# A fused decoder block: four row blocks normalised in place and transposed ahead of the last rows of the output projection

## The chip, the cores and the metric

The kernel runs on one core of one Trainium2 chip. The metric is device microseconds of one execution. The times come from three executions of the kernel before; the profile comes from one further execution, whose own time is given beside its span.

## What is computed

The input is 1024 tokens of width 1024 in float32. The block adds two attention branches (a sliding-window one and a top-k one) behind sigmoid gates, multiplies the mix by a 1024 x 1024 output projection, adds that to the residual, and then runs a gated feed-forward layer of hidden width 2816 and a last norm. The part that matters here, from the reference:

```python
    mixed = gate_a * (o_a @ w_branch_a[l]) + gate_b * (o_b @ w_branch_b[l])
    h = h + mixed @ w_out[l]
    hn = rms_norm(h, ffn_norm_g[l])
    h = h + (jax.nn.silu(hn @ w_ffn_gate[l]) * (hn @ w_ffn_up[l])) @ w_ffn_down[l]
y = rms_norm(h, final_norm_g)
```

## The kernel before

**Numbers and products.** Each float32 operand is split into a high part (a cast, on ACT) and a low part (a subtraction, on DVE or POOL), and each product is three matmuls: high x high, high x low, low x high (`mm3`, L203, whose matmul is recorded as L194). The three large products of the block's second half use Strassen-Winograd: each operand is cut in four quadrants, and seven products m1 to m7 of quadrants or of sums of quadrants take the place of eight.

**The output projection** (`phase_mix`, L1169, and `winograd`, L1215). Its seven products run in the order m1, m5, m6, m3, m2, m7, m4. A product has 48 matmuls of 128 x 512: four chunks k of the inner dimension, four row blocks i of 128 tokens, three matmuls each. The accumulators are PSUM banks: m2 and m5 take the four banks of the pool `sp` (tile `s`), the others the four of `mm` (tile `ps`). When a row block has its last chunk, DVE adds the bank into `h1` (L1254). For all but m4 the loop has k outside and i inside, so that the four row blocks end together; for m4 it has i outside, so that row blocks 4, 5, 6 and 7 end one after the other. The operand parts of m4's left side lie in `fhl` (four buffers), those of the right side in `th` and `tl` (five each).

**The norm between the two layers.** `done` (L1198) is called when half a row of `h1` is final. It calls `squares` (L1264), which squares 512 columns on ACT with a running sum; the squared values themselves go to a scratch tile that nobody reads and that has the tag `fs`, the two buffers that `ffn_hidden` uses for its sums of weights. When the second half is done (row blocks 0 to 3 after m2, 4 to 7 in m4), it stores the row block to DRAM (L1201, the feed-forward layer's residual), and calls `norm_scaled` (L1283): `row_scale` (L1270) makes the factor of each token with a tiny DVE instruction, a power on POOL and two more tiny DVE instructions, and ACT scales the row block into `xs` (L1288), which has two buffers. `norm_transposed` (L1290), called one row block late, transposes `xs` on PE in eight 128 x 128 pieces into two `s` banks (L1297), and DVE multiplies each bank by the norm's gain into the feed-forward layer's quadrants `hb11`, `hb21` (tokens 0 to 511) or `hb12`, `hb22` (tokens 512 to 1023) (L1300). After m4, the row blocks still pending are transposed (L1211).

**The feed-forward layer** (`phase_ffn`, L1303, `ffn_hidden`, L1364). DVE first forms the quadrant sums t1 to t4 in four cuts of 128 tokens (L1319 to L1324). Then eleven rounds q of `ffn_hidden` each do seven products for the gate and the up matrix. `product` (L1396) takes weight parts (`weight`, L1377: cast L1392 on ACT, low part L1393 on DVE for q = 0 and on POOL later), then the operand parts (`operand`, L1342: four casts L1350 on ACT, four subtractions L1351 on DVE, made once and kept), then 24 matmuls. The first product is quadrant 11 in two `s` banks, the second quadrant 21 in two `ps` banks. The low part of quadrant 11 goes into the tile `spare`, that of quadrant 21 into the room of `hb11` itself (L1316), so it can be written only when t1, which reads `hb11` (L1321), is complete.

**What sets the order.** Each engine runs its own list of instructions in order. The kernel's text gives only the dependences and the program order; the lists are written by a scheduler that runs a model of the time while it compiles, and puts on each engine what it takes to be ready. `issue_after(x)` tells it that the instructions in the block must stand behind x in the list of x's engine; it is an order and makes no wait of its own.

Of the kernel before, what the change touches and what calls it, by code (L numbers as in the profile page):

```python
# [7 lines left out]
F32 = mybir.dt.float32  # L8
# [11 lines left out]
P = 128  # L20
D = 1024
KC = D // P
T = 1024
NB = T // P
# [79 lines left out]
class Program:  # L104
# [1064 lines left out]
    def phase_mix(self):  # L1169
        nc, I = self.nc, self.I  # L1170

        self.act_dram = {nm: [self.dr.tile([P, 512], F32, name=f"act{nm}_{k}") for k in range(NF // 2)]
                         for nm in ("11", "12", "22", "s1", "s2", "s3", "s4")}
        self.h1_dram = [self.dr.tile([P, D], F32, name=f"h1_dram{b}") for b in range(NB)]
        self.f_es, mes = ExitStack(), ExitStack()
        self.B, self.xs = {}, {}
        self.fwp = self.f_es.enter_context(self.pool("fwp"))
        xp = mes.enter_context(self.pool("mixed"))

        X, W = self.X, self.W = [{ij: xp.tile([P, 4, 512], F32, name=f"{nm}{ij}") for ij in ("11", "12", "21", "22")} for nm in "xw"]  # L1180
        for m in range(KC):
            nc.scalar.copy(X[f"1{m // 4 + 1}"][:, m % 4], self.mixed[m])
        with self.pool("merge", side="right") as gp:
            self.branch_b(1, gp)
        self.xh_es.close()
        self.psum(4, 4, 0, 0)
        bp = self.f_es.enter_context(self.pool("fb", side="right"))
        for ij in ("11", "21", "12", "22"):
            self.B[ij] = bp.tile([P, 4, 512], F32, name=f"hb{ij}", tag=f"b{ij}", bufs=1)
        self.bp = bp  # L1190
        hp = mes.enter_context(self.pool("h1", side="right"))
        self.open_h1(hp)
        for b in range(NB):
            with self.tc.issue_after(self.mixed_in):
                nc.sync.dma_start(self.h1[:, b, :], I["x"][0][P * b:P * b + P, :])
        self.rp = mes.enter_context(self.pool("ring", side="right"))

        def done(b, nh):  # L1198
            self.squares(b, nh)
            if nh == 0:  # L1200
                nc.sync.dma_start(self.h1_dram[b], self.h1[:, b, :])  # L1201
                self.norm_scaled(b)
                self.pending.append(b)
                if len(self.pending) > 1:
                    self.norm_transposed(self.pending.pop(0))

        self.pending = []
        banks = lambda name: [(self.sp if name in ("m2", "m5") else self.mm).tile(
            [P, 512], F32, name="s" if name in ("m2", "m5") else "ps", tag="s" if name in ("m2", "m5") else "ps") for _ in range(4)]
        self.winograd(X, W, 4, ("m1", "m5", "m6", "m3", "m2", "m7", "m4"), banks, done)  # L1210
        while self.pending:  # L1211
            self.norm_transposed(self.pending.pop(0))
        mes.close()

    def winograd(self, a, b, kc, order, banks, done=None):  # L1215

        nc = self.nc
        a, b, sums = dict(a), dict(b), {}  # L1220

        def combine(d, name, dst, x, y, op):
            for k in range(kc):
                nc.vector.tensor_tensor(d[dst][:, k], d[x][:, k], d[y][:, k], op=op)
            d[name] = d[dst]

        sub, plus = ALU.subtract, ALU.add
        for at, name in enumerate(order):
            if name == "m5":
                combine(a, "s1", "21", "21", "22", plus)  # L1230
                combine(b, "t1", "12", "12", "11", sub)
            elif name == "m6":
                combine(a, "s2", "s1", "s1", "11", sub)
                combine(b, "t2", "t1", "22", "t1", sub)
            elif name == "m3":
                combine(a, "s3", "11", "22", "s2", sub)
                combine(b, "t3", "11", "t2", "11", sub)
                combine(a, "s4", "s2", "12", "s2", sub)
                combine(b, "t4", "t2", "t2", "21", sub)
            an, bn, old, to = WINOGRAD[name]  # L1240
            ps4 = sums[name] = sums[old] if old else banks(name)
            ops = []
            rows = name == "m4" and done
            for k in range(kc):
                ops.append((self.parts(a[an][:, k], self.fwp, ("fhl",), 4, False), self.parts(b[bn][:, k], self.rp, ("th", "tl"), NTH, False)))
            for k, i in [(k, i) for i in range(4) for k in range(kc)] if rows else [(k, i) for k in range(kc) for i in range(4)]:
                c = slice(P * i, P * i + P)
                x, y = ops[k]
                self.mm3(ps4[i], [(x[0][:, c], x[1][:, c], *y)], start=not old and k == 0, stop=k == kc - 1, skip_group_check=bool(old))
                if k < kc - 1:  # L1250
                    continue
                for half, nh, op in to:
                    h = self.h1[:, 4 * half + i, 512 * nh:512 * nh + 512]
                    nc.vector.tensor_tensor(h, h, ps4[i], op=op)  # L1254
                    if done and (name, half, nh) in (("m3", 0, 1), ("m2", 0, 0), ("m7", 1, 1), ("m4", 1, 0)):
                        done(4 * half + i, nh)
# [4 lines left out]
        self.h1 = hp.tile([P, NB, D], F32, name="h1")  # L1261
        self.ss = hp.tile([P, NB, 2], F32, name="ss")

    def squares(self, b, nh):  # L1264

        ss = self.ss[:, b, nh:nh + 1]
        junk = self.fwp.tile([P, 512], F32, name="sq", tag="fs", bufs=2)
        self.nc.scalar.activation(junk, self.h1[:, b, 512 * nh:512 * nh + 512], AF.Square, accum_out=ss)

    def row_scale(self, b):  # L1270
# [12 lines left out]
    def norm_scaled(self, b):  # L1283

        nc = self.nc
        r = self.row_scale(b)
        x = self.xs[b] = self.hp.tile([P, D], F32, name="xs", tag="xs", bufs=2)
        self.scaled_act = nc.scalar.activation(x, self.h1[:, b, :], AF.Copy, scale=r).ins  # L1288

    def norm_transposed(self, b):  # L1290

        nc, x = self.nc, self.xs[b]
        gcol = self.col["ffn_norm_g"]
        for kh in range(2):
            pt = self.sp.tile([P, 512], F32, name="s", tag="s")
            for k in range(4):
                nc.tensor.transpose(pt[:, P * k:P * k + P], x[:, 512 * kh + P * k:512 * kh + P * k + P], self.ident)  # L1297
            g = self.vec[:, gcol + 4 * kh:gcol + 4 * kh + 4]
            dst = self.B[f"{kh + 1}{b // 4 + 1}"]
            nc.vector.tensor_mul(dst[:, :, P * (b % 4):P * (b % 4) + P], pt.rearrange("p (k t) -> p k t", k=4),  # L1300
                                 g.unsqueeze(2).to_broadcast([P, 4, P]))
# [40 lines left out]
    def operand(self, name):  # L1342

        nc, hi = self.nc, self.Bhi[name]
        if name not in self.Blo:
            raw = self.B[name]
            pool, tag = next(self.places)
            lo = self.Blo[name] = pool.tile([P, 4, 512], F32R, name=f"l{name}", tag=tag, bufs=1)
            for k in range(4):
                nc.scalar.copy(hi[:, k], raw[:, k])  # L1350
                nc.vector.tensor_sub(lo[:, k], raw[:, k], hi[:, k].bitcast(F32))  # L1351
        return hi, self.Blo[name]

# [10 lines left out]
    def ffn_hidden(self, ap, q):  # L1364


        nc, I, wp = self.nc, self.I, self.fwp
        raws = [{}, {}]
# [25 lines left out]
            return hi, lo  # L1394

        def product(wname, bname, banks=None):  # L1396
            w = [weight(a, wname) for a in raws]
            first = banks is None
            if first:
                self.turn = not self.turn  # L1400
                pool, tag = (self.sp, "s") if self.turn else (self.mm, "ps")
                banks = [pool.tile([P, 512], F32, name=tag, tag=tag) for _ in range(2)]
            hi, lo = self.operand(bname)
            for k in range(4):
                for ps, (wh, wl) in zip(banks, w):
                    self.mm3(ps, [(wh[:, k], wl[:, k], hi[:, k], lo[:, k])], start=first and k == 0, stop=k == 3,
                             skip_group_check=not first)
            return banks
# [14 lines left out]
        def swiglu(pair, name, gate=None):  # L1423
# [4 lines left out]
            if name != "21":  # L1428
                nc.sync.dma_start(self.act_dram[name][q], act[name])

        x = product("11", "11")
        p1 = copies(x)
        swiglu(added(p1, product("12", "21")), "11")
        product("s2", "t2", x)
        u2 = copies(x)
        y = product("s1", "t1")
# [155 lines left out]
```

## Time and profile before

| | |
|---|---|
| Time of three executions | 1464.68, 1469.76, 1470.12 us, median 1469.76 |
| Time of the profiled execution | 1467.04 us |
| Its span in the trace | 1465.3 us, 21198 instructions |
| Its mean granted TensorE clock | 0.979 |
| Busy share | PE 94%, DVE 68%, ACT 56%, POOL 43% |

Of the times in the trace, 0 is the start of the span. m7 ends and the first transposes begin at 788.27 us, the last matmul of m4 starts at 802.73 us, and the first product of the feed-forward layer starts at 817.91 us. A busy PE is a stream of matmuls whose records overlap: the spacing from start to start is what counts, 0.23 us for a 128 x 512 one at full clock.

### The profile page before, as it was taken

Reading aid. Unit: us, or ns where it says so; the run is one execution under the profiler, and the core shown is the slowest. Engines: PE = TensorE matmul, PEld = TensorE weight load, DVE = VectorE, ACT = ScalarE, POOL = GpSimd, SP = SyncE. Lnnn points to the kernel's source line nnn. Section 1 sums busy time; section 2 is a strip of 40 time slices with the busy share of each in tenths; the row PEclk is TensorE's granted clock in tenths of the full one; section 3 lists DMA queues with packets and bytes.
Section 4 is the critical chain, followed back from the end, with each engine's and each line's share of the span. In section 5 each row is a group of like instructions: output and inputs, shape, how many; then the busy total and the mean of one; then the engine's idle time right before and its main releaser. Section 6 shows DMA issues by size and latency. Waiting matters only on the chain.

```text
span 1465.3 us, 21198 instructions
## 1 busy us (share of the span) xinstructions
PE 1380.8 (94%) x6847; PEld 1150.7 (79%) x6847; DVE 991.8 (68%) x2013; ACT 817.3 (56%) x1743; POOL 635.0 (43%) x895
## 2 busy tenths in 40 slices
PE   4999999986998999999899799999999999999997
PEld 3888988764876879898677678888888888888886
DVE  6257937959786797786797975444454447696593
ACT  5337987973786787884246633333333333444473
POOL 4225567474575666664101035555555554000005
PEclk9999999997998899999999899999999999999999
DMA  6511231463337564337902042333332328823332
GB/s 200 166 51 44 59 88 65 166 200 93 109 98 188 152 177 135 120 108 255 334 13 103 13 135 103 108 115 108 108 107 84 107 99 316 308 101 108 118 106 115
DMA packets 148038, 189.79 MB, mean 130 GB/s; under 512 B 11331, under 2 KB 95126, under 8 KB 147670
## 3 DMA queue, kind: packets, MB, share of 16 engines
q1 hardware_dynamic: 147568, 188.28, 39.7%
q8 instruction: 54, 0.88, 0.2%
q14 instruction: 58, 0.48, 0.1%
q10 hardware_dynamic: 198, 0.14, 0.0%
q0 software_dynamic: 160, 0.01, 0.0%
HBM read 133.49 MB, written 58.03 MB: 131 GB/s over the span
## 4 chain that ended last, share of the span: by engine, by line
PE 72%; DVE 11%; ACT 5%; issue 4%; DMA 4%; POOL 4%; SPq 0%; POOLq 0%; DVEq 0%; ACTq 0%
PE ps L194 28%; PE s L194 24%; PE gps L194 10%; PE pv L1085 2%; PE tp L1074 2%; PE s L1043 2%; ACT mask L891 2%; PE tp L199 1%; DMA ga<-gate_dram 1%; PE pv L194 1%; PE pv L1088 1%; POOL mask L835 1%; DMA gt<-ya_dram 1%; DMA da<-act 1%; POOL y L1553 1%
## 5 line engine op out<-in xcount | busy, mean ns | idle before, releaser
L1393 POOL TENSOR_TENSOR fhl<-fs,fhl 128x512 fp32r<-128x512 f32 x80 | 106.8, 1356 | 106.3 <-ACT fhl L1392 106.3
L1393 POOL TENSOR_TENSOR fhl<-fr,fhl 128x512 fp32r<-128x512 f32 x60 | 96.4, 1625 | 118.9 <-ACT fhl L1392 75.8
L194 PE MATMUL s<-ht,fhl 128*128 128x512 f32 x384 | 121.9, 392 | 0.6 <-DVE fhl L1393 0.6
L189 POOL TENSOR_TENSOR w_lo<-w_raw,w_hi 128x512 fp32r<-128x512 f32 x60 | 81.4, 1358 | 71.2 <-ACT w_hi L188 60.3
L194 PE MATMUL ps<-ht,fhl 128*128 128x512 f32 x320 | 100.8, 391 | 0.0
L194 PE MATMUL gps<-oh,w_hi 128*128 128x512 f32 x232 | 94.8, 409 | 5.1 <-ACT gt L949 4.8
L194 PE MATMUL gps<-oh,w_lo 128*128 128x512 f32 x232 | 92.7, 400 | 0.0
L194 PE MATMUL gps<-ol,w_hi 128*128 128x512 f32 x232 | 92.7, 399 | 0.0
L1463 ACT CAST yhl<-wd 128x512 fp32r<-128x512 f32 x66 | 41.1, 623 | 89.3 <-PE ps L194 50.2
L194 PE MATMUL s<-yhl,fhl 128*128 128x512 f32 x396 | 90.6, 389 | 0.0
L194 PE MATMUL ps<-yhl,fhl 128*128 128x512 f32 x396 | 90.3, 389 | 0.0
L194 PE MATMUL s<-h,fhl 128*128 128x512 f32 x272 | 87.5, 393 | 0.8 <-DVE hb L1300 0.5
L133 DVE TENSOR_TENSOR ptl<-tp,pth 128x512 fp32r<-128x512 f32 (+2 forms) x112 | 71.0, 646 | 23.7 <-ACT pth L127 23.4
L194 PE MATMUL ps<-h,fhl 128*128 128x512 f32 x256 | 82.8, 394 | 4.4 <-ACT h L1350 4.4
L194 PEld LDWEIGHTS s<-yhl,fhl 128*128 128x128 f32 x396 | 74.3, 188 | 15.5
L194 PEld LDWEIGHTS ps<-yhl,fhl 128*128 128x128 f32 x396 | 74.3, 188 | 15.5
L194 PEld LDWEIGHTS s<-ht,fhl 128*128 128x128 f32 x384 | 72.0, 188 | 17.9 <-DVE fhl L1393 1.0
L1392 ACT CAST fhl<-fr 128x512 fp32r<-128x512 f32 x66 | 39.9, 620 | 74.4 <-issue 32.9
L1464 DVE TENSOR_TENSOR yhl<-wd,yhl 128x512 fp32r<-128x512 f32 x66 | 45.6, 691 | 48.8 <-ACT yhl L1463 48.8
L891 ACT ACTIVATE mask<-high,smallg 128x1040 bf16<-128x1040 uint16 (+2 forms) x66 | 71.5, 1083 | 11.4 <-DVE high L836 5.4
L194 PE MATMUL s<-lt,fhl 128*128 128x512 f32 x192 | 75.4, 393 | 0.0
L1392 ACT CAST fhl<-fs 128x512 fp32r<-128x512 f32 x88 | 54.8, 625 | 35.8 <-PE s L194 17.4
(505 smaller groups left out, 4217.8 us busy)
## 6 DMA issues: line engine op xcount, KB each, us to landing
fr<-in_w_ffn_gate SPq DMA_DIRECT2D x22, 512.0 KB, 3.9
fr<-in_w_ffn_up SPq DMA_DIRECT2D x22, 512.0 KB, 4.7
wd<-in_w_ffn_down SPq DMA_DIRECT2D x44, 256.0 KB, 4.2
da<-acts SPq DMA_DIRECT2D x44, 256.0 KB, 3.1
w_raw<-in_w_in SPq DMA_DIRECT2D x40, 256.0 KB, 3.2
act<-a SPq DMA_DIRECT2D x33, 256.0 KB, 2.1
da<-act SPq DMA_DIRECT2D x33, 256.0 KB, 2.9
acts<-s SPq DMA_DIRECT2D x33, 256.0 KB, 2.0
```

Source lines behind the costliest of these rows:

```text
L133: b = nc.vector.tensor_sub(lo, ps, hi.bitcast(F32))
L189: (nc.vector if lo_dve else nc.gpsimd).tensor_sub(t[1], t[2], t[0].bitcast(F32))
L194: mm = self.nc.tensor.matmul(*args, **kw)
L199: mm = self.nc.tensor.transpose(*args)
L891: nc.scalar.activation(self.mask[j], src[j], AF.Sign, bias=at[:, i:i + 1], scale=scale, accum_out=out[:, i:i + 1])
L1043: nc.tensor.matmul(ps[:, :n], q[k][:, h, qc:qc + P], kb[:, h, at:at + n], start=k == 0, stop=k == 1)
L1074: mm = nc.tensor.transpose(pt[:, P * i:P * i + P], prs[par, e][:, NM + P * rr:NM + P * rr + P], self.ident)
L1085: mm = nc.tensor.matmul(acc[:, e, :], v, t[k][:, 256 * i:256 * i + 256], start=r + i + k == 0, stop=False)
L1392: nc.scalar.copy(hi, a[name])
L1393: (nc.gpsimd if q else nc.vector).tensor_sub(lo, a[name], hi.bitcast(F32))
L1463: nc.scalar.copy(hi, src)
L1464: nc.vector.tensor_sub(lo, src, hi.bitcast(F32))
```

## The change

Row blocks 0 to 3 are scaled in place in `h1`; `xs` stays for row blocks 4 to 7. The pending row blocks are transposed (`flush`) before m4's matmuls are written, and the matmuls of m4's row blocks 5, 6 and 7 (i = 1 to 3) are ordered on PE behind the last of these transposes; row block 4 (i = 0) is left free. The scratch of `squares` becomes a buffer of its own in this phase. In round q = 0, for the quadrants 11 and 21, the operand parts are written before the weight parts, and the casts of the weights are ordered on ACT behind the last cast of the operand.

```diff
         def done(b, nh):
-            self.squares(b, nh)
+            self.squares(b, nh, self.hp)
...
         self.winograd(X, W, 4, ("m1", "m5", "m6", "m3", "m2", "m7", "m4"), banks, done)
+        self.flush()
+        mes.close()
+
+    def flush(self):
         while self.pending:
             self.norm_transposed(self.pending.pop(0))
-        mes.close()
...
             rows = name == "m4" and done
+            if rows:
+                self.flush()
...
-                self.mm3(ps4[i], [(x[0][:, c], x[1][:, c], *y)], start=not old and k == 0, stop=k == kc - 1, skip_group_check=bool(old))
+
+                with self.tc.issue_after(self.transposed) if rows and i else nullcontext():
+                    self.mm3(ps4[i],     [(x[0][:, c], x[1][:, c], *y)], start=not old and k == 0, stop=k == kc - 1, skip_group_check=bool(old))
...
-    def squares(self, b, nh):
+    def squares(self, b, nh, pool=None):
...
-        junk = self.fwp.tile([P, 512], F32, name="sq", tag="fs", bufs=2)
+        junk = (pool or self.fwp).tile([P, 512], F32, name="sq", tag="sq" if pool else "fs", bufs=2)
...
-        x = self.xs[b] = self.hp.tile([P, D], F32, name="xs", tag="xs", bufs=2)
+        x = self.xs[b] = self.h1[:, b, :] if b < NB // 2 else self.hp.tile([P, D], F32, name="xs", tag="xs", bufs=2)
...
-                nc.tensor.transpose(pt[:, P * k:P * k + P], x[:, 512 * kh + P * k:512 * kh + P * k + P], self.ident)
+                self.transposed = nc.tensor.transpose(pt[:, P * k:P * k + P], x[:, 512 * kh + P * k:512 * kh + P * k + P], self.ident).ins
...
-                nc.scalar.copy(hi[:, k], raw[:, k])
+                self.act_split = nc.scalar.copy(hi[:, k], raw[:, k]).ins
...
-            w = [weight(a, wname) for a in raws]
+
+            ahead = q == 0 and bname in ("11", "21")
+            if ahead:
+                self.operand(bname)
+            with self.tc.issue_after(self.act_split) if ahead else nullcontext():
+                w = [weight(a, wname) for a in raws]
```

## Rows read from the trace of the kernel before

**Rows 1.** The page's busy time of each engine over the span.
```profile
PE 1380.8 (94%) x6847; PEld 1150.7 (79%) x6847; DVE 991.8 (68%) x2013; ACT 817.3 (56%) x1743; POOL 635.0 (43%) x895
```

**Rows 2.** Busy us by stage: PE, PEld, DVE, ACT, POOL; granted clock, DMA share, GB/s.
```profile
788.00:803.40 15.40, 15.13 (x82) 12.38 (x80) 12.25 (x22) 8.02 (x17) 0.26 (x1) 1.00 0.11 43
803.40:846.20 42.80, 31.70 (x135) 24.58 (x135) 42.42 (x81) 30.27 (x55) 4.40 (x4) 0.88 0.16 57
846.20:1240.00 393.80, 393.80 (x1715) 322.12 (x1716) 206.59 (x241) 137.03 (x245) 203.15 (x140) 1.00 0.36 123
1240.00:1275.00 35.00, 35.00 (x154) 28.64 (x153) 22.86 (x37) 14.64 (x26) 0.00 (x0) 1.00 0.97 358
```

**Rows 3.** Waits of PE from 846 us to the end: waited for, total, times, longest.
```profile
PE s L194 <- DVE fhl L1393: 0.6, 1, 0.6
```

**Rows 4.** PE in order of time, 803 to 827 us: idle before and its releaser in brackets.
```profile
807.48 1.22 PE L194 MATMUL ps<-h,fhl 128*128 128x512 f32 x2 [4.35 <-ACT h L1350]
810.71 5.62 PE L1297 MATMUL s<-ident,xs 128*128 128x128 f32 x28 [2.00 <-ACT xs L1288]
...
817.91 0.50 PE L194 MATMUL s<-h,fhl 128*128 128x512 f32 x1 [0.54 <-DVE hb L1300]
...
826.92 0.50 PE L194 MATMUL ps<-l,fhl 128*128 128x512 f32 x1 [3.26 <-DVE l L1351]
```

**Rows 5.** Stages inside that stretch, the same columns as rows 2.
```profile
807.40:810.60 3.20, 1.22 (x2) 0.50 (x2) 3.20 (x11) 3.20 (x8) 1.19 (x1) 0.50 0.00 1
810.60:817.90 7.30, 6.28 (x32) 5.68 (x32) 6.92 (x15) 3.39 (x4) 0.87 (x1) 0.68 0.00 0
...
823.70:826.90 3.20, 0.00 (x0) 0.00 (x0) 3.20 (x7) 3.20 (x7) 0.00 (x0) 1.00 0.00 0
```

**Rows 6.** DVE in order of time, 770 to 829 us.
```profile
773.49 0.69 DVE L133 TENSOR_TENSOR fhl<-x,fhl 128x512 fp32r<-128x512 f32 x1 [4.84 <-ACT fhl L127]
...
778.89 0.68 DVE L1254 TENSOR_TENSOR h<-h,s 128x512 f32<-128x512 f32 x1
...
792.35 0.69 DVE L1300 TENSOR_TENSOR hb<-s,vec 128x512 f32<-128x512 f32 x1
...
798.60 0.69 DVE L1300 TENSOR_TENSOR hb<-s,vec 128x512 f32<-128x512 f32 x1 [3.15 <-PE s L1297]
...
826.18 2.49 DVE L1351 TENSOR_TENSOR l<-hb,h 128x512 fp32r<-128x512 f32 x4
```

**Rows 7.** PE in order of time, 788 to 803 us.
```profile
788.27 1.91 PE L1297 MATMUL s<-ident,xs 128*128 128x128 f32 x16
...
798.63 1.47 PE L1297 MATMUL s<-ident,xs 128*128 128x128 f32 x12
...
802.73 0.40 PE L194 MATMUL ps<-th,fhl 128*128 128x512 f32 x1
```

**Rows 8.** ACT in order of time, 783 to 801 us.
```profile
783.91 2.19 ACT L1288 ACTIVATE xs<-h,rh 128x1024 f32<-128x1024 f32 x2
...
789.40 1.15 ACT L1288 ACTIVATE xs<-h,rh 128x1024 f32<-128x1024 f32 x1 [0.32 <-PE s L1297]
...
799.98 0.63 ACT L1268 ACTIVATE sq<-h 128x512 f32<-128x512 f32 x1 [6.54 <-DVE h L1254]
```

**Rows 9.** DMA of the row blocks' stores (L1201): 770 to 830 us, us to landing.
```profile
h_dram<-h SPq DMA_DIRECT2D x8, 512.0 KB, 3.4
```

**Rows 10.** Instructions of tile fs: ns min/median/max, first and last start.
```profile
L1382 DVE TENSOR_TENSOR fs<-fr x2: 683/687/691, 806.3 to 810.4; 128x512 f32<-128x512 f32 x2
```

**Rows 11.** SP's queue: the fourth and last load of round 0's weights.
```profile
715.95 1.29 SPq L1373 DMA_DIRECT2D fr<-in_w_ffn_up  x1
```

**Rows 12.** The stage 738 to 750 us, the same columns as rows 2.
```profile
738.00:750.00 12.00, 12.00 (x53) 9.66 (x52) 12.00 (x21) 5.36 (x10) 0.00 (x0) 1.00 0.00 0
```

**Rows 13.** ACT groups, 770 to 850 us: busy us, mean ns.
```profile
L1288 ACT ACTIVATE xs<-h,rh 128x1024 f32<-128x1024 f32 x8 | 8.9, 1142 | 1.9 <-PE s L1297 1.9
```

**Rows 14.** POOL in order of time: the power of the last row block.
```profile
810.65 0.87 POOL L1277 TENSOR_TENSOR rh<-rh,power 128x1 f32<-128x1 f32 x1 [2.06 <-DVE rh L1276]
```

## The prediction

> **What bounds the kernel now.** I read the page's busy shares first: PE is busy 94% of the span, so the place to look for time is where PE is not [rows 1]. The stage table finds it. In the stage behind the change, 846.2 to 1240 us, PE is busy all the time, as it is from 1240 to 1275, and from 846 us to the end of the span only one wait of PE is on record, 0.6 us at its very start [rows 2, 3]. In the stretch that holds the transition from the output projection to the feed-forward layer, 803.4 to 846.2 us, PE is busy 31.70 of 42.80 us, while DVE is busy 42.42 [rows 2]. So the transition is worth at most 42.8 - 31.7 = 11.1 us of idle PE and what the clock costs there, and whatever moves 846 us earlier moves the end by the same amount.
>
> PE's timeline says which waits those are: 4.35 us for a cast of a quadrant, 2.00 us for a scaled row block, some 0.9 us for banks that DVE had to empty, and 3.26 us for the low part of quadrant 21, the last wait to end [rows 4]. The clock adds a little: it was granted 0.50 and 0.68 after the first of these waits [rows 5], that is partly its lower level of 1.2 GHz, and 28 transposes took (5.62 - 0.27) / 27 = 0.198 us each there [rows 4] against (1.91 - 0.27) / 15 = 0.109 at 788 us [rows 7], 0.27 being the last one's own length: 28 x 0.089 = 2.5 us. The ceiling of any change to this stretch is then 11.1 + 2.5 = 13.6 us, 0.9% of the time.
>
> DVE's timeline says who decides. DVE has a hole of 3.15 us before 798.60 us, where it waits for the transposes of row blocks 2 and 3, and from there it is busy almost without a break until the low part of quadrant 21, four subtractions from 826.18 us [rows 6, 2]. That low part can't move up by itself: it is written over quadrant 11, so it stands behind t1, which needs row block 7. So **the end of DVE's list sets the end of PE's wait**, and the question is how much of DVE's work in 798.6 to 826.2 can be put where DVE is idle now. One DVE instruction of 128 x 512 counts (2.49 - 0.69) / 3 = 0.60 us in a run [rows 6].
>
> **The change part by part.**
>
> *Transposes of row blocks 0 to 3 ahead of the last rows.* Nothing is added: the same 32 transposes, eight gains (L1300) and 48 matmuls of m4 run. The gains of row blocks 2 and 3 are four of the sixteen and run from 798.6 us now, because PE's list has their transposes behind most of m4 [rows 7], though the scaling of row block 2 began at 789.40 us [rows 8]. With them ahead of row block 5 the four gains fall into the hole before 798.6 us: **4 x 0.60 = 2.4 us gained** of its 3.15. If the hole only wanders to where DVE waits for m4's later rows, it is 0; more than 3.15 it can't be.
>
> *PE behind the last transpose.* What is queued behind it is 36 matmuls of row blocks 5 to 7. The transposes need four `s` banks twice, so those of row blocks 2 and 3 wait for the gains of 0 and 1, which run on DVE from 792.35 us, behind the last additions of m7 [rows 6]. Three more and one low part of m4 between them, at 0.60, make the fourth bank free at about 795.4, and the last transpose ends at about 795.9. A matmul takes 393.8 / 1715 = 0.23 us in a full stream [rows 2], so the last of the 36 starts 35 x 0.23 = 8.05 us later, at about 803.95, against 802.73 now [rows 7]. PE pays 1.2 us in m4. It is covered by DVE's list, which is still the later of the two, and costs nothing unless it grows past the 2.4 us gained. The Trainium skill ("TensorE: Matmul & The Clock Gate", Part 3, The mechanism) says that matmuls start and end strictly in the order of the program, so none of the 36 could step around a waiting transpose; if they could, the 1.2 us would be nothing, and no run here shows which. I count them as held.
>
> *Scaling in place.* The third scaling waited 0.32 us for a transpose that read its buffer [rows 8]; that wait goes. What comes instead: a row block may be overwritten only when its store has been read out. The store takes 3.4 us [rows 9], and the last of the four row blocks is final on DVE at 778.89 + 0.68 = 779.6 us [rows 6], so the last store is through at about 783.0, before the first scaling of now, 783.91 us [rows 8]. Cost nothing; the cover is the chain of factors on DVE and POOL, and without it up to 3.4 us for the first row block. No DMA is added, and none changes its place in SP's queue by more than that.
>
> *Scratch of the squares.* Today the first sums of weights (L1382 and L1383, two instructions each, 0.60 us in a run) can't be written before the squares of the last rows leave the `fs` buffers, and stand from 806.3 us on, in the middle of DVE's full stretch [rows 10]. Their inputs are loaded long before: the last load was issued at 715.95 us, and from 738 to 750 us no DMA ran [rows 11, 12]. With `fs` free they can use the rest of the hole or the one of 4.84 us before 773.49 [rows 6]. Between 0 (the scheduler leaves them) and 4 x 0.60 = 2.4 us; I take 2.4, since nothing else claims these holes.
>
> *Casts ordered apart.* The eight casts of quadrants 11 and 21 can run in ACT's gap of 6.54 us before 799.98 [rows 8] instead of behind 803, where PE waits 4.35 us for one of them [rows 4]. The weights' casts, queued behind them, need `fhl` buffers that m4 frees only in its last row block, so they lose nothing. This shortens a chain that is not the last to end: after m4's end, row block 7 needs an addition of 0.68, a square of 0.63 [rows 8] with its read-out, the power of 0.87 [rows 14] with the tiny DVE work beside it, a scaling of 1.14 [rows 13], eight transposes (0.9 to 1.6) and two gains (1.3): 5.5 to 8 us, so it could be through at about 811, where the first product waits for a gain until 817.91 now [rows 4]. DVE's list behind it is longer than that. Alone 0, with a free DVE up to 8.
>
> *What is late next.* With the first product done at about 816, PE would wait for the low part of quadrant 21 longer than the 3.26 us of now, and the clock, which stayed at 1.00 through that wait [rows 5], may fall as it did after the 4.35 us. That costs between 0 and the 2.5 us found above; half of it can hide in DVE's list, and I take 0.8.
>
> Sum: 2.4 + 2.4 - 0.8 = **4.0 us gained**. The profiled execution took 1467.04 us, 2.7 under the median of 1469.76; on it the sum gives 1463.0, on the median 1465.8. The forecast is for the median: **1465.8 us**.
>
> **The rivals.**
>
> *The gain is two or three times that.* If the scheduler also puts the low part of quadrant 21 ahead of the sums t2 and t3 (eight instructions of 0.60 stand before it now), PE gets it 4.8 us earlier still: 4.0 + 4.8 = 8.8, 1461.0 us, with 13.6 as the limit, 1456.2. For it: row block 4 is free to finish before the transposes end, so that gains and sums for it can fill DVE in m4. Against it: t1 to t4 stand first in the program.
>
> *The hole wanders.* DVE finishes the gains early and then waits for m4's later rows, which end later than now; only the sums of weights are gained, and the clock takes most of that: 0 to 1.5 us, 1469 us. For it: between 798 and 804 us DVE would have only the additions, the tiny instructions and little else. This is also the case in which the scheduler's lists come out nearly as before.
>
> *Slower.* If DVE's list has five more instructions ahead of the gains of row blocks 0 and 1 (low parts of m4, the addition of row block 4, sums of weights), the fourth bank comes 5 x 0.60 = 3.0 us later, at 798.4. PE is out of work when the first 16 transposes and the 12 matmuls of row block 4 are done, at 788.27 + 1.7 + 12 x 0.23 = 792.7, and idles for most of 5.7 us, more than the 4.35 after which the clock fell [rows 4, 5], and the 36 matmuls start at the lower clock. The transposes ran 0.198 / 0.109 = 1.8 times as long there, which makes 0.42 us of a matmul's 0.23. The low clock lasted until the stage that ends at 817.9, some 10 us, so 20 of the 36 are 0.19 longer, 4 us: m4's last matmul starts at 798.9 + 8.05 + 4 = 811, 8 us late. Of DVE's tail 2.4 to 4.8 us has gone, so the low part of quadrant 21 comes 3.2 to 5.6 us later than now: 1473 to 1475.5 us, and more if DVE idles meanwhile. It decides from the point where m4 ends more than 4.8 us late. The strict order of matmuls that the Trainium skill states ("TensorE: Matmul & The Clock Gate", Part 3, The mechanism) would let none of the 36 run in that gap. Against it: the same gains ran at 792.35 in the present list.
>
> **How the numbers follow.** About 0.5% is what a measurement of this kernel can tell from no change: 7.3 us. Forecast 0.5 (1463 to 1468), larger gain 0.2, hole that wanders 0.2, slower 0.1. Faster by over 0.5% is under 1462.4: most of the larger gain, 0.17, and the low end of the forecast, 0.07, together 0.24. Slower by over 0.5% is over 1477.1: 0.06 of the last. Within: 0.70. The range takes in the larger gain down to 1458.5 and the wandering hole with the spread of three runs up to 1471.5.
>
> **What would show it.** Right: all 32 transposes of row blocks 0 to 3 between 788 and 796 us, no DVE hole before 798, m4's end at 804 to 805, the first sums of weights before 800, casts of quadrant 11 near 798, and a first low part of quadrant 21 at 821 to 823 with PE waiting for it. Wrong: that low part at 818 or earlier (larger gain); an idle DVE between 798 and 804 (the hole wandered); an idle PE of over 4 us with a clock under 0.8 between 788 and 804 (slower). A PE that waits again behind 846 us would break the premise that the rest only shifts.

## The result, and the profile after

| | before | after |
|---|---|---|
| Median (range, executions) | 1468.62 us (1462.1 to 1470.12, 9) | 1474.17 us (1472.51 to 1482.55, 9) |
| Ratio | | 1.0058, 95% interval 1.0043 to 1.0073 |
| Profiled execution | 1467.04 us, span 1465.3 | 1477.76 us, span 1476.0 |
| First transpose of the norm to the end of the span | 1465.3 - 788.27 = 677.0 us | 1476.0 - 789.85 = 686.2 us |

The change makes the kernel slower by 0.6%: the means of the executions lie 8.5 us apart (1475.74 and 1467.25), the medians 5.6. The last row is the measure used from here on, "the stretch to the end": the time ahead of the first transpose runs from 783.77 us (x6) to 790.90 us (x9) in the traces, though these two kernels have the same edits there. By it the change loses 9.1 us. It comes from one profiled execution of each kernel; beside the timed ratios it is off by up to 2.5 us (worst for x11 below), so differences smaller than that are not read from it alone.

Page of the kernel after, busy time of each engine (as [rows 1]):

```profile
PE 1384.0 (94%) x6847; PEld 1152.5 (78%) x6847; DVE 992.9 (67%) x2013; ACT 817.2 (55%) x1743; POOL 633.5 (43%) x895
```

The same instructions run, in nearly the same busy time. What changed is who waits. The stages of the kernel after, with the columns of [rows 2]; the first three are the same stretches, the fourth is the 58 us that begin at the first transpose, the fifth is discussed below:

```profile
788.00:803.40 15.40, 12.06 (x65) 9.00 (x63) 13.81 (x27) 7.61 (x18) 1.10 (x2) 0.98 0.13 52
803.40:846.20 42.80, 28.12 (x114) 22.34 (x115) 32.62 (x59) 24.79 (x46) 2.02 (x2) 0.77 0.08 31
846.20:1240.00 393.80, 393.58 (x1713) 321.13 (x1713) 203.92 (x247) 140.40 (x250) 197.79 (x136) 1.00 0.34 115
...
789.85:847.85 58.00, 39.98 (x178) 31.23 (x177) 46.22 (x85) 32.18 (x62) 3.12 (x4) 0.82 0.09 37
...
804.10:809.00 4.90, 4.90 (x16) 4.22 (x17) 1.38 (x2) 0.99 (x1) 0.00 (x0) 0.50 0.00 0
```

and the same 58 us of the kernel before:

```profile
788.27:846.27 58.00, 46.63 (x216) 36.89 (x214) 54.46 (x101) 38.02 (x71) 4.66 (x4) 0.91 0.14 54
```

PE idles 58.00 - 39.98 = 18.0 us there, against 58.00 - 46.63 = 11.4 before: 6.65 us more. Its mean granted clock is 0.82 against 0.91, and what is left of the loss, 9.1 - 6.65 = 2.5 us, is put down to PE's work running slower; that is an estimate. Behind 846 us PE is full in both, so the loss is made in this stretch and only passed on. The second thing to see is DVE: it was busy 42.42 of 42.80 us [rows 2] and is now busy 32.62. The engine that was to set the end has itself 10 us of idle time.

PE in order of time, kernel after (as [rows 4] and [rows 7]; L1304 are the transposes, and "xs" is a row block from 4 to 7):

```profile
789.85 1.91 PE L1304 MATMUL s<-ident,h 128*128 128x128 f32 x16
...
795.88 1.25 PE L1304 MATMUL s<-ident,h 128*128 128x128 f32 x8
...
804.10 1.97 PE L1304 MATMUL s<-ident,xs 128*128 128x128 f32 x8 [3.93 <-ACT xs L1295]
...
810.40 1.03 PE L1304 MATMUL s<-ident,xs 128*128 128x128 f32 x8
...
813.84 0.40 PE L194 MATMUL ps<-th,fhl 128*128 128x512 f32 x1
815.07 1.09 PE L1304 MATMUL s<-ident,xs 128*128 128x128 f32 x8 [0.83 <-ACT xs L1295]
820.77 1.32 PE L194 MATMUL ps<-h,fhl 128*128 128x512 f32 x2 [4.61 <-ACT fhl L1399]
...
830.35 1.97 PE L1304 MATMUL s<-ident,xs 128*128 128x128 f32 x8 [8.26 <-ACT xs L1295]
```

Row blocks 0 to 3 went as forecast: their last transposes end at 797.1 us, 7.3 after the first (7.6 were forecast). Then something that no step of the prediction has: the transposes of row block 4 stand in PE's list *between* m4's row blocks 5 and 6, those of row block 5 between 6 and 7. At 804.10 PE has waited 3.93 us for row block 4 to be scaled, with the 24 matmuls of row blocks 6 and 7 queued behind. Their operands were complete (the last low part of m4 starts on DVE at 796.34).

The edit itself puts the transposes there. Its order reads `self.transposed` anew for each row block, and `norm_transposed` writes that variable. When row block 5 is written, `done` calls `norm_transposed` for row block 4, so row block 6 is ordered behind the transposes of row block 4, and in the same way row block 7 behind those of row block 5. The section on the change says of all three row blocks that they stand behind the last transpose of row block 3; that holds for row block 5 alone. Without the order (the kernel before, x1, x4, x8, x11) the scheduler leaves the transposes of row blocks 4 to 7 behind m4.

m4's last matmul starts at 813.84 instead of 802.73 [rows 7]. The last wait, 8.26 us, is for row block 7, behind two matmuls of the feed-forward layer.

The chain of waits of the kernel after, 796 to 833 us (start, us, what), shows both parts at once:

```profile
797.13 2.82 PE ps L194 x12
...
799.97 0.70 DVE h L1261
...
800.75 0.73 ACT sq L1275 x2
...
801.87 0.56 POOL rh L1284
...
802.90 1.16 ACT xs L1295
...
804.10 1.97 PE s L1304 x8
806.07 4.49 PE ps L194 x12
810.56 0.87 PE s L1304 x8
811.43 2.82 PE ps L194 x12
...
814.28 0.69 DVE h L1261
...
826.39 0.14 DVE rh L1283
...
829.15 1.16 ACT xs L1295
...
830.35 1.97 PE s L1304 x8
```

**Part one, inside m4.** The chain is addition, square, tiny instructions with the power on POOL, scaling, transposes: about 4.1 us from 799.97 to 804.10, and PE has nothing else that its list lets it do. The clock falls: 804.10 to 809 us is granted 0.50, the level of 1.2 GHz. The price is in the same rows: 12 matmuls take 4.49 us at 806.07 and 2.82 at 811.43, eight transposes 1.97 and 0.87; 1.67 + 1.10 = 2.8 us.

**Part two, row block 7.** Its addition starts at 814.28, its transposes at 830.35, 16.1 us later, where the prediction gave a chain of 5.5 to 8 us to the end of its gains. ACT in order of time, kernel after, says what stood ahead of its square:

```profile
814.92 2.16 ACT L1357 CAST h<-hb 128x512 fp32r<-128x512 f32 x4
816.99 1.13 ACT L1399 CAST fhl<-fr 128x512 fp32r<-128x512 f32 x2
818.03 2.17 ACT L1357 CAST h<-hb 128x512 fp32r<-128x512 f32 x4
820.11 1.13 ACT L1399 CAST fhl<-fr 128x512 fp32r<-128x512 f32 x2
821.15 0.63 ACT L1275 ACTIVATE sq<-h 128x512 f32<-128x512 f32 x1
```

Twelve casts, so the square comes at 821.15, 6.2 us after the addition has ended. Then its first tiny instruction waits in DVE's list behind sums and low parts until 826.31, and the chain of waits from 814.28 to there runs along DVE's list. DVE in order of time, kernel after:

```profile
826.31 0.20 DVE L1283 TENSOR_SCALAR rh<-ss 128x1 f32<-128x1 f32 x1
```

### The profile page after: what moved, and what is told of

It is laid out like the page before. It is cut to its first block, busy times and chain, and to the rows that moved or that the text cites. A ratio compares the mean times of both kernels' runs of the same rounds, so it can differ in the third digit from the quotient of the medians.

```text
span 1476.0 us, 21181 instructions
## 1 busy us (share of the span) xinstructions
PE 1384.0 (94%) x6847; PEld 1152.5 (78%) x6847; DVE 992.9 (67%) x2013; ACT 817.2 (55%) x1743; POOL 633.5 (43%) x895
## 4 chain that ended last, share of the span: by engine, by line
PE 73%; DVE 9%; ACT 5%; DMA 5%; issue 4%; POOL 4%; SPq 1%; POOLq 0%; ACTq 0%; DVEq 0%
PE ps L194 28%; PE s L194 26%; PE gps L194 9%; PE pv L1085 2%; PE s L1043 2%; PE tp L1074 2%; ACT mask L891 2%; DMA ga<-gate_dram 1%; PE tp L199 1%; PE pv L194 1%; DVE pa L749 1%; POOL mask L835 1%; DVE ptl L133 1%; POOL y L1565 1%; PE pv L1088 0%
## 5 line engine op out<-in xcount | busy, mean ns | idle before, releaser
L1284 POOL TENSOR_TENSOR rh<-rh,power 128x1 f32<-128x1 f32 x16 | 11.0, 699 | 144.4 <-DVE rh L1283 144.4
```

## The experiments

Two theories after the trace. **Row order**: ordering m4's row blocks 5 to 7 behind the transposes is the loss, through part one and part two; the other edits cost nothing. **Casts** (the rival): ordering the first weights' casts behind the operands' casts puts them ahead of row block 7's square, so that edit is the loss. All kernels compute the whole reference. "Ratio" is the time over that of the kernel before on the same chip, with its 95% interval; "stretch" is from the first transpose to the end, 677.0 before and 686.2 with the change.

**x1, the change without the row order.**

```diff
-                with self.tc.issue_after(self.transposed) if rows and i else nullcontext():
-                    self.mm3(ps4[i],     [(x[0][:, c], x[1][:, c], *y)], start=not old and k == 0, stop=k == kc - 1, skip_group_check=bool(old))
+                self.mm3(ps4[i], [(x[0][:, c], x[1][:, c], *y)], start=not old and k == 0, stop=k == kc - 1, skip_group_check=bool(old))
```

> The changed kernel without the order that puts the matmuls of m4's row blocks 5 to 7 behind the last transpose of row block 3; all else stays. Theory ORDER (that order lets the transposes of row blocks 4 to 6 stand between m4's row blocks in PE's list, so that PE waits in the middle of m4 for a scaling that can't be ready): the loss goes, ratio 0.996 to 1.002, no wait of PE for xs before m4's last matmul, which starts at 802 to 805 us. Theory CASTS (the eight casts of quadrants 11 and 21 and the four of the weights stand ahead of row block 7's square on ACT): most of the loss stays, ratio 1.004 to 1.008, a wait of 6 to 9 us for the last xs.

Measured: ratio 1.0008 (0.9993 to 1.0022), stretch 676.7. PE in order of time:

```profile
806.12 1.32 PE L194 MATMUL ps<-h,fhl 128*128 128x512 f32 x2 [5.44 <-ACT fhl L1397]
808.30 6.58 PE L1302 MATMUL s<-ident,xs 128*128 128x128 f32 x32 [0.87 <-ACT xs L1293]
```

The whole loss goes. The transposes of row blocks 4 to 7 stand together behind m4, as before. And the other three edits together bring nothing that can be measured.

Twelve casts stand ahead of row block 7's square here too, with no loss. The square, and the last tiny instruction of that row block, on ACT and DVE:

```profile
806.49 0.63 ACT L1273 ACTIVATE sq<-h 128x512 f32<-128x512 f32 x1
```

```profile
808.50 0.16 DVE L1284 SCALAR_TENSOR_TENSOR rh<-rh 128x1 f32<-128x1 f32 x1
```

From the square's start to the finished factor takes 2.2 us here and 7.9 us with the change (821.15 to 829.05). So the casts by themselves are not part two. What x1 lacks is the gains and sums of row blocks 4 to 6 in DVE's list ahead of the tiny instructions; they came forward with the transposes of these row blocks.

**x2, the change without the order of the casts.**

```diff
-            ahead = q == 0 and bname in ("11", "21")
-            if ahead:
-                self.operand(bname)
-            with self.tc.issue_after(self.act_split) if ahead else nullcontext():
-                w = [weight(a, wname) for a in raws]
+            w = [weight(a, wname) for a in raws]
```

> The changed kernel with operand and weight parts in the old order. Theory ORDER: m4 is still cut in pieces, a wait of 3 to 5 us for xs inside m4, ratio 1.003 to 1.008. Theory CASTS: row block 7's square comes within 2 us of its addition, the wait of 8.26 us is under 3, ratio 0.997 to 1.002.

Measured: ratio 1.0070 (1.0049 to 1.0091), stretch 686.3. The waits for row block 4 and row block 7 are still there, 3.93 and 8.14 us. Twelve casts of weights and operands stand ahead of row block 7's square without this edit too. The rival falls: with or without it, the loss is there.

**x3, the kernel before with the row order alone** (and the `flush` that it needs; no scaling in place, no scratch, no order of casts).

```diff
+            if rows:
+                self.flush()
...
+                with self.tc.issue_after(self.transposed) if rows and i else nullcontext():
...
```

> The kernel before with only the early flush and the order on m4's row blocks 5 to 7: xs in two buffers, scratch in fs, casts as before. Theory ORDER: slower alone, ratio 1.003 to 1.009, PE waits inside m4. Theory CASTS: same as before, 0.998 to 1.002.

Measured: ratio 1.0073 (1.0052 to 1.0094), stretch 687.4. PE in order of time:

```profile
798.14 1.78 PE L1303 MATMUL s<-ident,xs 128*128 128x128 f32 x8 [2.63 <-ACT xs L1294]
...
824.01 1.97 PE L1303 MATMUL s<-ident,xs 128*128 128x128 f32 x8 [11.04 <-ACT xs L1294]
```

The row order alone makes the whole loss, with waits in the same two places, 2.63 and 11.04 us. The four kernels that have it and still call the transposes of row blocks 4 and 5 inside m4 (the change, x2, x3, x9) all wait there.

**x4, the kernel before with the squares' own scratch alone.**

```diff
-            self.squares(b, nh)
+            self.squares(b, nh, self.hp)
```

> The kernel before with only the squares' scratch in a buffer of its own. By the prediction's term the four first sums of weights leave DVE's full stretch: 0 to 2.4 us gained, ratio 0.998 to 1.000, first sums before 800 us. If the scratch costs (a tile that shifts others), 1.001 or more.

Measured: ratio 1.0001 (0.9989 to 1.0014), stretch 676.6. Tile `fs` (ns min/median/max, first and last start), and then PE's last wait:

```profile
L1382 DVE TENSOR_TENSOR fs<-fr x22: 677/694/1691, 725.2 to 1208.0; 128x512 f32<-128x512 f32 x22
```

```profile
828.98 0.50 PE L194 MATMUL ps<-l,fhl 128*128 128x512 f32 x1 [2.69 <-DVE l L1351]
```

The first sums of weights did leave DVE's full stretch, for 725 us, where they began at 806.3 [rows 10]. Of the 2.4 us that they free, PE gets 0.57 back: 3.26 us [rows 4] became 2.69. Most of the rest is new idle time of DVE. Two stretches with the columns of [rows 2], both from 15.28 us after the first transpose on, x4 and then the kernel before:

```profile
806.00:829.00 23.00, 12.63 (x59) 9.80 (x59) 21.00 (x45) 15.77 (x30) 3.30 (x4) 0.85 0.15 60
```

```profile
803.55:826.55 23.00, 13.25 (x58) 10.61 (x58) 22.62 (x48) 15.97 (x30) 4.25 (x4) 0.78 0.15 61
```

DVE idles 2.00 us in x4 and 0.38 before; it waits 0.35 us for a square, 0.73 for a power and 0.86 for transposes.

**x5, the change with the transposes of row blocks 4 to 7 ordered behind m4's last matmul.**

```diff
-                if len(self.pending) > 1:
+                if b < NB // 2 and len(self.pending) > 1:
...
-        self.flush()
+        with self.tc.issue_after(self.last_row):
+            self.flush()
...
-                    self.mm3(ps4[i],     [(x[0][:, c], x[1][:, c], *y)], start=not old and k == 0, stop=k == kc - 1, skip_group_check=bool(old))
+                    self.last_row = self.mm3(ps4[i], [(x[0][:, c], x[1][:, c], *y)], start=not old and k == 0, stop=k == kc - 1, skip_group_check=bool(old))
```

> The whole change, and the transposes of row blocks 4 to 7 ordered on PE behind m4's last matmul, so that none stands between m4's row blocks. Theory ORDER, in the form that the transposes between the rows cost: no wait of PE for xs before m4's last matmul, which starts at 803 to 806 us after a first transpose at 788; a wait for the last xs of 3 to 6 us stays, because the squares of row block 7 stand behind twelve casts on ACT; from the first transpose to the end 676 to 680 us (677.0 before, 686.2 with the change). If instead the 36 matmuls behind row block 3's transposes are what costs: 684 us or more.

With it `self.transposed` stays at the last transpose of row block 3 through all of m4, so row blocks 5 to 7 are ordered as the prediction had it. Measured: ratio 1.0022 (1.0012 to 1.0033), stretch 680.5. m4 is whole again, and 5.6 of the 9.1 us are back. PE, and then ACT, in order of time:

```profile
822.26 1.97 PE L1304 MATMUL s<-ident,xs 128*128 128x128 f32 x8 [5.34 <-ACT xs L1295]
```

```profile
813.15 0.63 ACT L1275 ACTIVATE sq<-h 128x512 f32<-128x512 f32 x1
...
821.06 1.15 ACT L1295 ACTIVATE xs<-h,rh 128x1024 f32<-128x1024 f32 x1 [6.16 <-DVE rh L1286]
```

What is left is part two: row block 7's square still stands behind twelve casts, its factor is ready 7.8 us after the square's start (2.2 in x1), and its transposes are waited for.

**x6, x5 with the casts of the operands ordered behind the last scaling on ACT.**

```diff
-            for k in range(4):
-                self.act_split = nc.scalar.copy(hi[:, k], raw[:, k]).ins
-                nc.vector.tensor_sub(lo[:, k], raw[:, k], hi[:, k].bitcast(F32))
+            with self.tc.issue_after(self.scaled_act):
+                for k in range(4):
+                    self.act_split = nc.scalar.copy(hi[:, k], raw[:, k]).ins
+                    nc.vector.tensor_sub(lo[:, k], raw[:, k], hi[:, k].bitcast(F32))
```

> As x5, and the casts of the feed-forward layer's operands ordered on ACT behind the last scaling, so that row block 7's square goes first. The wait for the last xs goes under 2 us; from the first transpose to the end 672 to 676 us, ratio 0.994 to 0.999. If DVE's list sets the end alone: 677, as before.

Measured: ratio 0.9984 (0.9973 to 0.9995), stretch 675.8. The rest of the loss goes, and the kernel is faster than before, by 0.16%; x7 and x10, which contain these edits, have intervals that reach past 1. PE in order of time:

```profile
809.43 1.97 PE L1304 MATMUL s<-ident,xs 128*128 128x128 f32 x8 [5.51 <-ACT xs L1295]
```

The wait for row block 7 was expected under 2 us and is no shorter than in x5, but it ends 25.7 us after the first transpose (at 783.77 us) instead of 32.6 (822.26 - 789.66), since none of the operands' casts stands ahead of it.

**x9, the change with only the second of these repairs**: the casts behind the last scaling, as in x6, and the transposes of row blocks 4 and 5 still inside m4, where the order of the change puts them.

```diff
-            for k in range(4):
-                self.act_split = nc.scalar.copy(hi[:, k], raw[:, k]).ins
-                nc.vector.tensor_sub(lo[:, k], raw[:, k], hi[:, k].bitcast(F32))
+            with self.tc.issue_after(self.scaled_act):
+                for k in range(4):
+                    self.act_split = nc.scalar.copy(hi[:, k], raw[:, k]).ins
+                    nc.vector.tensor_sub(lo[:, k], raw[:, k], hi[:, k].bitcast(F32))
```

> The whole change, with the transposes of row blocks 4 to 7 left free to stand between m4's rows as in the change, and only the casts of the operands ordered behind the last scaling on ACT. If the loss is two separate things (PE held by a transpose inside m4, and row block 7's chain behind casts), this repairs the second alone: PE still waits 3 to 4 us for a scaling inside m4, the wait of row block 7's transposes falls from 8.3 to 4 to 6 us, first transpose to end 680 to 683 us (before 677.0, the change 686.2), ratio 1.002 to 1.004. If the order on ACT is all that was wrong, it comes out as x6 did: 675 to 677 us, ratio 0.998 to 1.000. If transposes inside m4 are all that was wrong, 685 to 687 us.

Measured: ratio 1.0042 (1.0027 to 1.0056), stretch 681.8. PE in order of time:

```profile
805.15 1.97 PE L1303 MATMUL s<-ident,xs 128*128 128x128 f32 x8 [3.94 <-ACT xs L1294]
...
823.26 1.97 PE L1303 MATMUL s<-ident,xs 128*128 128x128 f32 x8 [7.05 <-ACT xs L1294]
```

By the stretches these are two separate losses: this repair alone gives 4.4 us, x5's alone 5.6, together 10.0, and x6 has 10.3. By the ratios it is less clear: the two give 2.3 and 5.3 us, x6 10.9, and the interval of x9 overlaps that of the change. The wait of 7.05 us was expected at 4 to 6: the square now starts at 815.04, but DVE's list still holds the tiny instructions back until 821.79.

**x7, x6 with t1 of all four cuts and the operands 11 and 21 written ahead of t2 to t4.**

```diff
+        self.operand("11")
+        self.operand("21")
+        for at, n in CUTS:
+            cut = {nm: B[nm][:, :, at:at + n] for nm in B}
...
```

> As x6, and t1 of all four cuts and the operand parts of quadrants 11 and 21 written ahead of t2, t3 and t4 in the program. If DVE's list is what PE waits for at the second product, 1 to 3 us better than x6 and a wait for the low part of quadrant 21 under 3 us; if the time is set by row block 7's chain, the same as x6.

Measured: ratio 0.9992 (0.9978 to 1.0006), stretch 675.2. PE's wait for row block 7 is the same 5.51 us, and a wait of 2.70 us for a cast of a weight comes behind it. No gain over x6.

**x8, x1 with room of its own for the casts of quadrant 11** (they are written to a tile whose room is given out when the projection's pools close), and four buffers instead of five for `th` and `tl` to make that room.

```diff
-NTH = 5
+NTH = 4
...
+        self.h11 = bp.tile([P, 4, 512], F32R, name="h11", tag="h11", bufs=1)
...
```

> As x1 (no row order), with the high part of quadrant 11 placed in the pool that is open during the projection, and the ring of th and tl cut from five to four buffers to make the room. Theory ROOM: the casts of quadrant 11 could not be scheduled ahead of m4's last matmul because their tile lies in the room of the projection's pools, handed out only when those close. Then here they run before 801 us where in x1 they run after 801; the time stays within 0.3% of x1, since the second product still waits for the low part of quadrant 21. If ROOM is wrong, the casts stay behind 801 us.

Measured: ratio 1.0008 (0.9998 to 1.0019), stretch 678.6. ACT in order of time:

```profile
801.45 2.18 ACT L1357 CAST h<-hb 128x512 fp32r<-128x512 f32 x4 [7.85 <-DVE hb L1306]
```

The casts start 12.5 us after the first transpose instead of 14.4 in x1 (800.26 - 785.83), right behind the gains that they need. So room was worth 2 us of lateness, and PE's time nothing. The expectation was a start before 801 us here and behind 801 us in x1; from the start of the span neither came true (801.45 and 800.26).

**x10, x6 with the sums t1 to t4 ordered on DVE behind row block 7's last tiny instruction.**

```diff
+        with self.tc.issue_after(self.scaled_dve):
+            for at, n in CUTS:
...
```

> x6 with the sums t1 to t4 ordered on DVE behind row block 7's last tiny instruction as well. In x6 that chain waits in DVE's list behind sums, and its transposes wait 5.5 us on PE. If DVE's order is the rest of that wait, it falls below 2.5 us, first transpose to end 672 to 675 us, ratio 0.995 to 0.998. If the sums that are put off come back as a later wait for t1's parts or a low part (the rival), that wait grows by 2 to 4 us and the time stays at x6's: 675 to 677 us, ratio 0.998 to 1.000.

Measured: ratio 0.9991 (0.9979 to 1.0002), stretch 675.7. PE in order of time, then two stages with the columns of [rows 2]:

```profile
808.23 1.78 PE L1304 MATMUL s<-ident,xs 128*128 128x128 f32 x8 [1.96 <-ACT xs L1295]
...
817.51 1.22 PE L194 MATMUL s<-h,fhl 128*128 128x512 f32 x2 [2.26 <-DVE fhl L1402]
```

```profile
802.00:808.20 6.20, 3.26 (x25) 2.57 (x24) 5.85 (x14) 4.30 (x7) 0.55 (x1) 1.00 0.46 183
808.20:822.50 14.30, 10.59 (x27) 6.97 (x28) 14.30 (x25) 11.24 (x22) 0.00 (x0) 0.52 0.00 0
```

The wait for row block 7 falls from 5.51 to 1.96 us, so DVE's order was most of what was left of it. The time does not follow: the low part of a weight, put off on a DVE that is busy all of the 14.30 us, is late by 2.26, and PE's work there runs at a granted clock of 0.52.

**x11, the kernel before with only the casts behind the last scaling.**

```diff
-            for k in range(4):
-                nc.scalar.copy(hi[:, k], raw[:, k])
-                nc.vector.tensor_sub(lo[:, k], raw[:, k], hi[:, k].bitcast(F32))
+            with self.tc.issue_after(self.scaled_act):
+                for k in range(4):
+                    nc.scalar.copy(hi[:, k], raw[:, k])
+                    nc.vector.tensor_sub(lo[:, k], raw[:, k], hi[:, k].bitcast(F32))
```

> The kernel before with only the casts of the operands ordered behind the last scaling on ACT; no row order, no own scratch, no scaling in place. If what x6 won comes from the chain's place on ACT alone, this gives it too: 674 to 676.5 us from first transpose to end, ratio 0.997 to 0.9995. If it needs the early transposes or the free scratch of the change, 676.5 to 679 us, ratio 0.9995 to 1.002.

Measured: ratio 0.9990 (0.9976 to 1.0003), stretch 678.0. The interval overlaps both expectations; the ratio itself is on the side of a gain, the stretch on the side of none. Whether x6's 0.16% needs the early transposes stays open.

## Why the prediction was wrong

The forecast was 1465.8 us and a gain of 4.0; the change is 0.58% slower, so the direction and the range were wrong, and "slower" had a chance of 0.1, slower by over 0.5% one of 0.06.

- **The step that failed is "PE behind the last transpose".** It says that what is queued behind the transposes "is 36 matmuls of row blocks 5 to 7" and that "PE pays 1.2 us in m4". That price is right for row blocks 0 to 3 (last transpose 7.3 us after the first). But only 12 of the 36 matmuls are queued there. The order takes its anchor from a variable that `norm_transposed` writes again inside m4, so row blocks 6 and 7 are queued behind the transposes of row blocks 4 and 5, each behind a chain of four engines. That costs 3.93 us of waiting, all of it for row block 4, and 2.8 us of lower clock, and m4's last matmul starts 24.0 us after the first transpose (813.84 - 789.85) instead of 14.5 (802.73 - 788.27). x5 takes these transposes out of m4 alone, and 5.6 us come back; x3 shows that the row order by itself puts them there. No run keeps the anchor at row block 3 and leaves the transposes of row blocks 4 and 5 free.
- **"Casts ordered apart" was right on its price and wrong on the chain.** The edit costs and gains nothing that can be measured (x1, x2). The casts did not run in ACT's gap ahead of m4's end either; against x1, x8 puts 2 us of that down to the room of their tile. But "a chain that is not the last to end", with row block 7 through at about 811 us, failed: it was costed as if ACT and DVE would run each of its steps at once. Twelve casts and a run of DVE work stand ahead of it in two lists, with m4 whole (x5) as with m4 cut up, and it ends last. With the casts alone ahead of it there is no loss (x1); with the casts put behind it the stretch is 4.4 us shorter (x9; 2.3 us by the ratio, not clear of the noise), and DVE's list still holds it. How much belongs to either list stays open. The trace of the kernel before already had a chain longer than the sum. Row block 7's addition on DVE and its scaling on ACT, kernel before:

```profile
804.11 0.69 DVE L1254 TENSOR_TENSOR h<-h,ps 128x512 f32<-128x512 f32 x1
```

```profile
814.47 1.15 ACT L1288 ACTIVATE xs<-h,rh 128x1024 f32<-128x1024 f32 x1 [0.56 <-PE s L1297]
```

  That is 10.4 us from the start of one to the start of the other, with the transposes and gains still to come, where 5.5 to 8 us were given for all.
- **"The end of DVE's list sets the end of PE's wait" held before and only in part after.** The gains of row blocks 2 and 3 fell into the hole, as said: they are through at 799.4 us, and the largest hole ahead of them from 787 us on is 1.21 us. DVE in order of time, kernel after:

```profile
787.95 4.87 DVE L1261 TENSOR_TENSOR h<-h,ps 128x512 f32<-128x512 f32 x8 [1.21 <-PE ps L194]
...
796.94 2.47 DVE L1307 TENSOR_TENSOR hb<-s,vec 128x512 f32<-128x512 f32 x4
```

  The hole did not close, it moved: DVE then waits for m4's late row blocks, and idles 42.80 - 32.62 = 10.2 us where it was full, before its list holds PE up again from 814.28 on, as the chain of waits shows. That is the rival "the hole wanders", and more.
- **The two gains of 2.4 us were over-sized even without the loss.** The scratch alone has a ratio of 1.0001 (x4), and scratch, scaling in place and order of casts together 1.0008 (x1). x6, with both gains, the loss repaired and the casts put last, has 0.9984, some 2.3 us of the 4.8. A DVE that is busy 42.42 of 42.80 us was not the only limit: when 2.4 us left its list, it idled 1.6 us more for a square, a power and transposes, and PE's wait shrank by 0.57 us (x4).
- **Scaling in place at nothing: right.** The four scalings run as one block of 4.27 us from 785.50, and x1 has them without a loss.
- **"What is late next", 0.8 us for the clock, was too small**: by the estimate above 2.5 us more than before.
- **The rival "slower" had the size, 1473 to 1475.5 us, not the place.** It has PE wait for banks ahead of the last transposes of row blocks 0 to 3; inside m4 PE's only long idle stretch is 3.93 us behind them. Its step from an idle PE to the lower clock and a late m4 is what happened.
- **The rule that was cited holds here.** The Trainium skill ("TensorE: Matmul & The Clock Gate", Part 3, The mechanism) has matmuls start and end strictly in program order, and the prediction had no row for it. Now there is one: at 804.10 PE had waited 3.93 us for eight transposes with 24 ready matmuls behind them, and none stepped around. Had they done so, they would have filled the wait (an estimate: 24 x 0.23 = 5.6 us).

## What to carry to other kernels

An order hint holds what its anchor variable names at that moment. Where a loop places the hint several times and the same loop writes the variable, each piece gets another anchor: write down for each piece which instruction it stands behind, and give that instruction the length of the chain it waits for. When the last part of a stage feeds a chain over several engines, cost that chain by its place in each engine's list and not by the sum of its steps, and look in the trace of the kernel before for how long it takes there. The two faults here came from one edit, and repairing one of them gave back 5.6 of 9.1 us (x5), so a repair that gives back a part is no sign of a wrong theory. And an engine that is busy 99% of a stretch need not be its only limit: work taken out of its list can turn into idle time (x4).

## What the runs showed of the hardware that was not expected

The granted clock fell where no wait was long. In x10 the longest wait of PE ahead of the fall is 1.96 us; PE was busy 3.26 of the 6.20 us before it, and the next 14.3 us were granted 0.52, close to the level of 1.2 GHz, though PE was busy 10.59 us of them. In the kernel before, the fall came within a single wait of 4.35 us: the clock was granted 1.00 from 803.40 to 805.10 us and 0.50 from there on, and the wait ended at 807.48 [rows 4]. So in this case breaking a long wait into short ones did not keep the clock, and of the 3.5 us that x10 saves on one wait nothing reached the end.
